# Down projection of a two-layer decoder trunk: first pass in half units with one pair at its end, second pass with its squares behind the next unit's parts, and the scale row on SP's queue

## Chip, core and metric

The kernel runs on one core of one Trainium2 chip, as one program and one launch. The metric is the device time of that launch in microseconds (us); lower is better. The core's engines are PE (matmuls; PEld is its weight load), DVE (vector), ACT (scalar), POOL (GpSimd) and SP, which here only issues DMAs. Each engine takes its own instructions in order, and semaphores tie the engines together.

## The reference, cut to what matters

Two layers, 512 tokens of width 1024, all in float32. Layer 0 mixes tokens by trailing means, layer 1 by attention over a window of 128 keys; after each stands the same feed-forward part, and this is what the change touches:

```python
def rms_norm(x, g):
    y = xf * lax.rsqrt(jnp.mean(xf * xf, axis=-1, keepdims=True) + RMS_EPS)
    return y * g

def conv_glu_ffn(h, w_in, conv_w, conv_b, w_out):      # h: (512, 1024)
    u = h @ w_in                                       # (512, 5632)
    up = jnp.pad(u, ((0, 0), (CONV_WIDTH - 1, 0), (0, 0)))
    u = sum(conv_w[k] * up[:, k:k + S] for k in range(3)) + conv_b
    gate, val = jnp.split(u, 2, axis=-1)
    return (gelu(gate) * val) @ w_out                  # (512, 2816) @ (2816, 1024)

for layer in range(2):
    h = rms_norm(x, mix_pre_g[layer])
    if layer == 0:
        m = pool_mixer(h, w_pool, pool_scale)          # ends with: y * scale, a row of 1024
    else:
        m = attention(h, ...)
    x = x + rms_norm(m, mix_post_g[layer])
    x = x + rms_norm(conv_glu_ffn(rms_norm(x, ffn_pre_g[layer]), ...), ffn_post_g[layer])
```

## The kernel before, in words

**Every product is three matmuls.** A float32 operand is cut into a high part (a copy to the format fp32r, on ACT) and a low part (the operand minus the high part, on DVE). `mm3` (L322 to L325) then issues high by high (L323), one low by high (L324) and the other low by high (L325). So each block of weights that lands in a buffer `raw` needs a cast on ACT (`wh`, L236) and a subtraction on DVE (`wl`, L237) before PE may use it. `split(i)` does this for weight unit i in two halves of 1024 columns and then asks SP to load units i+1 and i+2 into the two `raw` buffers. Three slots hold `wh`/`wl`; a few units of the second pass have a slot of their own (`homes`).

**The feed-forward part of a layer** runs in three stages. `first` makes the up projection for 22 column blocks j: 48 matmuls each, then `act(j)`, in which `conv` runs on ACT (L540) and DVE (L541, L542) for the gate half `tg`, then Gelu on ACT (L549), then `conv` for the value half `tv`, then their product (L556). Two blocks make a pair p; there are 11 pairs.

The down projection multiplies by a scheme of seven products in place of eight. Sums of quarters of the activations (`g_sums`) and of the weights (`w_sums`, written to DRAM as `t`) are made on POOL during `first`. **`pass1`** makes the products named 1, 6, 5 and 7, eight PSUM banks in all. Pair p uses unit `U_D1 + p` (four blocks of 512 columns, one for each product) and the activation parts `gh`, `gl` of `split1(p)`: a subtraction on DVE (L580), a cast on ACT (L582, `gh`), a subtraction on DVE (L583, `gl`). `gh` and `gl` rotate through five buffers `w4`, so `gl` of pair p+2 takes the buffer of `gh` of pair p. The loop runs over pairs 0 to 8 (`NP - NT` with `NT = 2`): `split1(p + 2)`, 24 matmuls, then `ahead(U_D1 + p)`, which splits unit p+2. The last two pairs stand together: product 1 of pairs 9 and 10, then product 6 of both, and so on.

**`pass2`** makes product 4 (three units m, 11 pairs) and then products 3 and 2 (six units, 11 pairs, the last three pairs one bank after the other). `soon(k)` splits the k-th of these nine units and makes its activation parts (`split2`, L654 on ACT and L655 on DVE). Between them stand the sums `Z` on DVE (L670, L722), the squares for the norm on ACT (`square_of`, L255), their sum and root on POOL (`root`), the gains on DVE (L697) and the new residual (`update`, L707). In layer 0 the norm of the next layer's input follows for blocks 2 and 3 (`pre_a`, `pre_b`) and their transposes on PE (`to_attention`).

**At the start**, the row of 1024 pool scales is loaded into partition 0 of a buffer `row` that DVE has filled with zeros (L88), and four matmuls with ones (L355) spread it over the partitions. The DMA is issued on ACT's queue (L333), behind half of `band`. Blocks x0 and x1 of the input are loaded by SP and normed by ACT, DVE and POOL (L366 to L374) before PE pools them (L394 to L397).

PE, ACT, DVE and POOL run in the order in which the code is written; SP's order is chosen by the framework.

## Time and profile before

| what | value |
|---|---|
| three timed runs | 919.35, 920.88, 922.05 us (median 920.88) |
| profiled execution | 920.7 us, span 918.9 us: 1.8 us lie around the span |
| instructions on PE (matmuls) | 4700 |
| `pass1` of layer 0, `pass2` of layer 0 | from 280.25 us, from 341.99 us |
| attention stage | from 390.88 us |
| `pass1` of layer 1, `pass2` of layer 1 | from 805.61 us, from 866.48 us; last matmul ends at 911.5 us |

A row of the timeline reads: start in us, duration in us, engine, line, operation, what is written and from what, shapes, count, and in brackets the idle time of that engine ahead of it with what ended the idle time. The end of a matmul is modelled in this profile: 128x512 matmuls that start 0.23 us apart are listed with 0.39 us each, so a busy PE is read by the distances between starts. In the prediction "layer 0" and "layer 1" are the two feed-forward parts, and units and pairs carry the numbers of the section above.

### The profile page before, as it was taken

How to read it: one execution, taken by the hardware profiler on the slowest of the kernel's cores; microseconds unless marked ns; L12 is line 12 of the kernel's file. 1: busy time of each engine (PE TensorE's matmuls, PEld its weight loads, DVE VectorE, ACT ScalarE, POOL GpSimd, SP SyncE). 2: the span in 40 equal slices, each digit the busy share in tenths (PEclk: the TensorE clock that was granted, in tenths of full speed). 3: DMA queues.
4: the chain of work that ended last, by engine and by line, in shares of the span. 5: the costliest groups of instructions: out<-in, count | busy, mean ns of one | idle time of the engine just before them, and what ended most of it. 6: DMA issues, size and time to landing. Idle time of an engine off the chain costs nothing.

```text
span 918.9 us, 12766 instructions
## 1 busy us (share of the span) xinstructions
PE 905.4 (99%) x4700; PEld 775.7 (84%) x4700; DVE 643.3 (70%) x958; ACT 465.2 (51%) x811; POOL 323.0 (35%) x371
## 2 busy tenths in 40 slices
PE   9999999999999999999999999999999999999996
PEld 8998888888887878799999889988888888888785
DVE  5878877677677777854888737655555555677877
ACT  5644444445344655554888634433433333455562
POOL 3415444444341000234767212544433333410001
PEclk9999999999999999999999999999999999999999
DMA  8356797888884655742112243455555555456643
GB/s 312 131 192 232 290 313 253 298 293 302 270 290 142 198 203 184 292 148 87 47 47 93 92 162 137 155 217 190 193 202 200 196 187 195 159 169 192 225 169 114
DMA packets 45184, 178.49 MB, mean 194 GB/s; under 512 B 5313, under 2 KB 6849, under 8 KB 36930
## 3 DMA queue, kind: packets, MB, share of 16 engines
q1 hardware_dynamic: 42720, 164.57, 50.9%
q10 hardware_dynamic: 2402, 13.11, 3.7%
q8 instruction: 37, 0.61, 0.3%
q14 instruction: 25, 0.20, 0.1%
HBM read 139.91 MB, written 37.75 MB: 193 GB/s over the span
## 4 chain that ended last, share of the span: by engine, by line
PE 82%; DVE 7%; issue 3%; DMA 3%; ACT 3%; POOL 2%; POOLq 0%; DVEq 0%; SPq 0%; ACTq 0%
PE u L325 17%; PE u L324 17%; PE u L323 17%; PE dn L324 4%; PE dn L325 4%; PE dn L323 4%; DVE wl L237 3%; DMA raw<-t 2%; PE qp L323 2%; PE qp L324 2%; PE qp L325 2%; PE op L323 2%; PE op L325 2%; PE op L324 2%; PE pT L929 1%
## 5 line engine op out<-in xcount | busy, mean ns | idle before, releaser
L323 PE MATMUL u<-xTh_f,wh 128*128 128x512 f32 (+1 forms) x768 | 285.7, 372 | 0.0
L324 PE MATMUL u<-xTl_f,wh 128*128 128x512 f32 (+1 forms) x768 | 285.2, 371 | 0.0
L325 PE MATMUL u<-xTh_f,wl 128*128 128x512 f32 (+1 forms) x768 | 285.2, 371 | 0.0
L237 DVE TENSOR_TENSOR wl<-raw,wh 128x1024 fp32r<-128x1024 f32 (+1 forms) x158 | 206.7, 1349 | 15.8 <-ACT wh L236 15.6
L541 DVE SCALAR_TENSOR_TENSOR t<-u,conv,t 128x511 f32<-128x511 f32 x88 | 65.8, 747 | 145.1 <-ACT t L540 145.1
L324 PEld LDWEIGHTS u<-xTl_f,wh 128*128 128x128 f32 x768 | 144.7, 188 | 25.1
L323 PEld LDWEIGHTS u<-xTh_f,wh 128*128 128x128 f32 x768 | 144.7, 188 | 24.9
L325 PEld LDWEIGHTS u<-xTh_f,wl 128*128 128x128 f32 x768 | 144.6, 188 | 24.8
L236 ACT CAST wh<-raw 128x1024 fp32r<-128x1024 f32 (+1 forms) x158 | 156.8, 1041 | 12.0 <-DMA raw<-t 7.5
L540 ACT ACTIVATE t<-u,conv 128x512 f32<-128x512 f32 x88 | 68.3, 777 | 139.0 <-PE u L325 104.9
L561 POOL TENSOR_TENSOR G<-G,G 128x256 f32<-128x256 f32 x22 | 33.4, 1516 | 266.2 <-DVE G L556 266.2
L324 PE MATMUL dn<-wl,gh 128*128 128x512 f32 x276 | 107.9, 391 | 1.8 <-DVE wl L237 1.8
L325 PE MATMUL dn<-wh,gl 128*128 128x512 f32 x276 | 107.8, 390 | 1.2 <-DVE gl L655 1.1
L323 PE MATMUL dn<-wh,gh 128*128 128x512 f32 x276 | 107.7, 390 | 0.0
L549 ACT ACTIVATE t<-t 128x512 f32<-128x512 f32 x44 | 27.8, 633 | 104.3 <-DVE t L542 104.3
L542 DVE SCALAR_TENSOR_TENSOR t<-u,conv,t 128x510 f32<-128x510 f32 x88 | 65.9, 749 | 3.1
L324 PEld LDWEIGHTS dn<-wl,gh 128*128 128x128 f32 x276 | 51.8, 188 | 14.0 <-DVE wl L237 3.4
L325 PEld LDWEIGHTS dn<-wh,gl 128*128 128x128 f32 x276 | 51.8, 188 | 12.9 <-DVE gl L655 2.4
L323 PEld LDWEIGHTS dn<-wh,gh 128*128 128x128 f32 x276 | 51.8, 188 | 11.0 <-ACT gh L654 0.3
L257 POOL TENSOR_SCALAR ss_p_f<-ss_p_f 128x1 f32<-128x1 f32 x8 | 3.2, 400 | 161.2 <-ACT dn L255 161.2
L582 ACT CAST gh<-G 128x1024 fp32r<-128x1024 f32 x22 | 23.1, 1051 | 56.0 <-DVE G L580 43.6
L583 DVE TENSOR_TENSOR gl<-G,gh 128x1024 fp32r<-128x1024 f32 x22 | 27.5, 1250 | 26.2 <-ACT gh L582 19.9
(199 smaller groups left out, 1517.5 us busy)
## 6 DMA issues: line engine op xcount, KB each, us to landing
raw<-in_ws_dram SPq DMA_DIRECT2D x48, 1024.0 KB, 5.0
q<-in_ws_dram SPq DMA_DIRECT2D x44, 512.0 KB, 6.4
raw<-t SPq DMA_DIRECT2D x24, 768.0 KB, 5.5
raw<-in_ws_dram SPq DMA_DIRECT2D x24, 512.0 KB, 4.6
t<-q SPq DMA_DIRECT2D x44, 256.0 KB, 3.0
t<-q SPq DMA_DIRECT2D x22, 512.0 KB, 3.0
r<-in_ws_dram SPq DMA_DIRECT2D x12, 512.0 KB, 6.9
hi<-h SPq DMA_DIRECT2D x12, 512.0 KB, 6.6
```

Source lines behind the costliest of these rows:

```text
L236: nc.scalar.copy(hi[:, s], r[:, s])
L237: nc.vector.tensor_tensor(lo[:, s], r[:, s], hi[:, s].bitcast(F32), ALU.subtract)
L323: nc.tensor.matmul(acc, ah, bh, start=first, stop=False)
L324: nc.tensor.matmul(acc, ah, bl, start=False, stop=False)
L325: nc.tensor.matmul(acc, al, bh, start=False, stop=last)
L540: nc.scalar.activation(t, u, AF.Identity, bias=conv_col(l, ch, 3), scale=conv_col(l, ch, 2))
L541: nc.vector.scalar_tensor_tensor(t[:, 1:], u[:, : S - 1], conv_col(l, ch, 1), t[:, 1:], ALU.mult, ALU.add)
L542: nc.vector.scalar_tensor_tensor(t[:, 2:], u[:, : S - 2], conv_col(l, ch, 0), t[:, 2:], ALU.mult, ALU.add)
L549: nc.scalar.activation(tg, tg, AF.Gelu_apprx_tanh)
L561: nc.gpsimd.tensor_tensor(s1, s1, G2[:, p, 2, :], ALU.add)
L582: nc.scalar.copy(h, G1[:, o : o + 1024])
L583: nc.vector.tensor_tensor(lo, G1[:, o : o + 1024], h.bitcast(F32), ALU.subtract)
```

## The change

Five edits; no instruction is added on PE, ACT, DVE or POOL.

- `split(i, between)` can call a function between its two halves. `split1(p, unit)` uses it: the order is now sum (L580), first half of the unit, `gh` and `gl`, second half of the unit, and all of it stands ahead of the 24 matmuls of pair p-2.
- `pass1` ends with one pair (`NT = 1`): pairs 0 to 9 run one after the other, and pair 10 alone stands at the end. `ahead` is gone from the loop.
- `conv` of the value half: the first step (ACT) of `tv` stands ahead of the Gelu of `tg`.
- `pass2`: the square of `Z22[m]` stands after `soon(m + 3)` in place of ahead of it; `soon(5)` stands ahead of the sums and squares of `Z21`, and `soon(6)` ahead of the gains.
- The DMA of the scale row is issued by SP, third in its queue, ahead of `cst`, x1 and the second part of `band`.

```diff
-    def split(i):
+    def split(i, between=None):
         if i in slots or i >= N_UNITS:
+            if between:
+                between()
             return
...
             nc.scalar.copy(hi[:, s], r[:, s])
             nc.vector.tensor_tensor(lo[:, s], r[:, s], hi[:, s].bitcast(F32), ALU.subtract)
+            if between and o == 0:
+                between()
...
+    nc.sync.dma_start(row[0:1], a["pool_scale"])
     nc.sync.dma_start(cst[:, :C_LATE], a["cst"][:, :C_LATE])
     nc.sync.dma_start(x[1], a["x"][1])
-    nc.scalar.dma_start(row[0:1], a["pool_scale"])
...
-        def conv(t, u, ch):
+        def conv(t, u, ch, then=lambda: None):
             nc.scalar.activation(t, u, AF.Identity, ...)
+            then()
...
             conv(tg, accs[j][0], j)
-            nc.scalar.activation(tg, tg, AF.Gelu_apprx_tanh)
-            conv(tv, accs[j][1], NF + j)
+            conv(tv, accs[j][1], NF + j, lambda: nc.scalar.activation(tg, tg, AF.Gelu_apprx_tanh))
...
-        def split1(p):
+        def split1(p, unit=None):
...
-            nc.scalar.copy(h, G1[:, o : o + 1024])
-            nc.vector.tensor_tensor(lo, G1[:, o : o + 1024], h.bitcast(F32), ALU.subtract)
+            def parts():
+                nc.scalar.copy(h, G1[:, o : o + 1024])
+                nc.vector.tensor_tensor(lo, G1[:, o : o + 1024], h.bitcast(F32), ALU.subtract)
+            if unit is None:
+                parts()
+            else:
+                split(unit, parts)
...
-        NT = 2
+        NT = 1
...
         for p in range(NP - NT):
-            split1(p + 2)
+            if p + 2 < NP:
+                split1(p + 2, U_D1[l] + p + 2)
             for q in of:
                 make(q, p)
-            ahead(U_D1[l] + p)
...
             soon(m + 2)
+            if m:
+                square_of("22", m - 1, 7)
             if m < 2:
                 nc.vector.tensor_tensor(Z["22"][m], Z["12"][m], X[7][m], ALU.add)
                 add("21", m, 7)
-                square_of("22", m, 7)
...
             if p == 0:
+                soon(5)
                 for i in range(2):
                     add("21", i, 4)
                     square_of("21", i, 4)
                     root(2 + i)
-                soon(5)
+                soon(6)
                 for i in range(2):
                     gain("21", i)
-                soon(6)
```

On PE, at the end of `pass1` of layer 0 (`dn_1_1` is the second bank of product 1, `dn_6_0` the first of product 6; `gh_9` and `gh_10` are the parts of pairs 9 and 10), there stood before:

```order
L325 MATMUL dn_1_1_2396<-wh_2698,gl_9_2671 128x512
L323 MATMUL dn_1_0_2395<-wh_2735,gh_10_2707 128x512
L324 MATMUL dn_1_0_2395<-wl_2736,gh_10_2707 128x512
L325 MATMUL dn_1_0_2395<-wh_2735,gl_10_2708 128x512
L323 MATMUL dn_1_1_2396<-wh_2735,gh_10_2707 128x512
```

and now stands:

```order
L330 MATMUL dn_1_1_2396<-wh_2672,gl_9_2671 128x512
L328 MATMUL dn_6_0_2397<-wh_2672,gh_9_2670 128x512
L329 MATMUL dn_6_0_2397<-wl_2673,gh_9_2670 128x512
L330 MATMUL dn_6_0_2397<-wh_2672,gl_9_2671 128x512
L328 MATMUL dn_6_1_2398<-wh_2672,gh_9_2670 128x512
```

The first use of pair 10 moved 18 matmuls back.

On ACT, in `pass2` of layer 0 from the parts of the last unit of product 4 (`gh_0_2` of 768 columns) on (`wh` rows are weight units, `gh_0_0` and `gh_0_1` the parts of the first two units of products 3 and 2, the `ACTIVATE` rows the squares), there stood before:

```order
L654 CAST gh_0_2_2867<-G_0_724 128x768
L255 ACTIVATE dn_7_0_2401,ss_p_f_2873<-Z_0_2797 128x512
L236 CAST wh_2900<-raw_2821 128x1024 x2
L654 CAST gh_0_0_2909<-G_0_724 128x1024
L255 ACTIVATE dn_7_1_2402,ss_p_f_2915<-Z_0_2797 128x512
L236 CAST wh_2936<-raw_2864 128x1024 x2
L654 CAST gh_0_1_2945<-G_0_724 128x1024
L255 ACTIVATE dn_4_0_2828,ss_p_f_2873<-Z_0_2797 128x512
L255 ACTIVATE dn_4_1_2829,ss_p_f_2915<-Z_0_2797 128x512
L236 CAST wh_2971<-raw_2906 128x1024 x2
L654 CAST gh_0_2_2980<-G_0_724 128x1024
```

and now stands:

```order
L666 CAST gh_0_2_2867<-G_0_724 128x768
L239 CAST wh_2897<-raw_2821 128x1024 x2
L666 CAST gh_0_0_2906<-G_0_724 128x1024
L260 ACTIVATE dn_7_0_2401,ss_p_f_2910<-Z_0_2797 128x512
L239 CAST wh_2933<-raw_2864 128x1024 x2
L666 CAST gh_0_1_2942<-G_0_724 128x1024
L260 ACTIVATE dn_7_1_2402,ss_p_f_2946<-Z_0_2797 128x512
L239 CAST wh_2963<-raw_2903 128x1024 x2
L666 CAST gh_0_2_2972<-G_0_724 128x1024
L260 ACTIVATE dn_4_0_2828,ss_p_f_2910<-Z_0_2797 128x512
L260 ACTIVATE dn_4_1_2829,ss_p_f_2946<-Z_0_2797 128x512
```

Each square moved behind one more unit's casts.

On DVE, in the loop of `pass1` of layer 0 (`gl_8` and `gl_9` are low parts of activations, `G_0` rows the sums of L580, `wl` rows the low parts of weight units 8 and 9), there stood before:

```order
L580 TENSOR_TENSOR G_0_728<-G_0_724,G_0_728 128x256
L583 TENSOR_TENSOR gl_8_2633<-G_0_728,gh_8_2632 128x1024
L237 TENSOR_TENSOR wl_2661<-raw_2590,wh_2660 128x1024 x2
L580 TENSOR_TENSOR G_0_728<-G_0_724,G_0_728 128x256
L583 TENSOR_TENSOR gl_9_2671<-G_0_728,gh_9_2670 128x1024
L237 TENSOR_TENSOR wl_2699<-raw_2628,wh_2698 128x1024 x2
```

and now stands:

```order
L585 TENSOR_TENSOR G_0_728<-G_0_724,G_0_728 128x256
L240 TENSOR_TENSOR wl_2635<-raw_2566,wh_2634 128x1024
L590 TENSOR_TENSOR gl_8_2633<-G_0_728,gh_8_2632 128x1024
L240 TENSOR_TENSOR wl_2635<-raw_2566,wh_2634 128x1024
L585 TENSOR_TENSOR G_0_728<-G_0_724,G_0_728 128x256
L240 TENSOR_TENSOR wl_2673<-raw_2604,wh_2672 128x1024
L590 TENSOR_TENSOR gl_9_2671<-G_0_728,gh_9_2670 128x1024
L240 TENSOR_TENSOR wl_2673<-raw_2604,wh_2672 128x1024
```

The low part of the activations moved between the two halves of the unit.

## The prediction, made before the run

> **What bounds the kernel now.** I read the page first, for the engine that carries the span, then PE's starts in the four stages that the change touches, then what DVE and ACT do where PE waits.
>
> ```profile
> span 918.9 us, 12766 instructions
> PE 905.4 (99%) x4700; PEld 775.7 (84%) x4700; DVE 643.3 (70%) x958; ACT 465.2 (51%) x811; POOL 323.0 (35%) x371
> PE 82%; DVE 7%; issue 3%; DMA 3%; ACT 3%; POOL 2%; POOLq 0%; DVEq 0%; SPq 0%; ACTq 0%
> ```
>
> PE carries 82% of the chain that ended last. No matmul is added or taken away, so time can only come out of stretches in which PE's starts are spread. The busy time by stretches, for the matmuls of the down projection alone, shows them: `pass1` and `pass2` of layer 0, then of layer 1.
>
> ```profile
> core 0: us, PE busy (x) PEld busy (x) DVE busy (x) ACT busy (x), PEclk, DMA share, GB/s
> 280.25:341.99 61.74, 60.68 (x264) 49.31 (x264) 1.28 (x2) 1.06 (x2) 1.00 0.59 189
> 341.99:390.88 48.89, 46.46 (x199) 36.52 (x197) 6.37 (x10) 4.12 (x12) 1.00 0.64 234
> 805.61:866.48 60.87, 60.16 (x265) 49.47 (x264) 1.28 (x2) 1.06 (x2) 1.00 0.56 188
> 866.48:911.40 44.92, 44.92 (x199) 36.97 (x197) 7.16 (x11) 4.96 (x14) 1.00 0.44 152
> ```
>
> The last row is dense: its 11 pairs are 198 matmuls (one more is counted at an edge), so one takes 44.92 / 198 = 0.2269 us, at a granted clock of 1.00. A `pass1` has 264 matmuls, 59.9 us when dense. It took 61.74 and 60.87: **1.84 and 0.97 us** are waits. `pass2` of layer 0 took 48.89, 3.97 more than its dense twin; two groups of transposes, 0.78 each, belong to it,
>
> ```profile
> 380.05 1.03 PE L316 MATMUL tr_a<-cst,xn_a 128*128 128x128 f32 x8
> 380.83 0.48 PE L323 MATMUL dn<-wh,gh 128*128 128x512 f32 x1
> ```
>
> which leaves **2.4 us**. Together 5.2 us is what the edits in the down projection can win at most, 0.57% of the kernel. Where it lies, from PE's timeline:
>
> ```profile
> 292.08 0.50 PE L324 MATMUL dn<-wl,gh 128*128 128x512 f32 x1 [0.35 <-DVE wl L237]
> 331.44 0.39 PE L323 MATMUL dn<-wh,gh 128*128 128x512 f32 x1
> 332.54 0.50 PE L324 MATMUL dn<-wl,gh 128*128 128x512 f32 x1 [0.71 <-DVE wl L237]
> 857.03 0.50 PE L324 MATMUL dn<-wl,gh 128*128 128x512 f32 x1 [0.71 <-DVE wl L237]
> 368.19 0.40 PE L324 MATMUL dn<-wl,gh 128*128 128x512 f32 x1
> 369.48 0.50 PE L325 MATMUL dn<-wh,gl 128*128 128x512 f32 x1 [0.89 <-DVE gl L655]
> 381.76 0.50 PE L325 MATMUL dn<-wh,gl 128*128 128x512 f32 x1 [0.21 <-DVE gl L655]
> ```
>
> Each is a wait for a low part from DVE. The second pair of rows shows how to read them: from start to start 1.10 us in place of 0.23, so 0.87 lost, though the bracket says 0.71. The brackets add up to 2.9 us, the starts to 5.2; I go by the starts. The Trainium skill (Perfetto Trace Analysis, section Identifying the Most-Contended Engine) tells the reader to find the gaps between slices of the bounding engine: by that rule the prize is 2.9 us and the sum below would end near 918, but the same page (section Per-instruction lifecycle) calls the end of a matmul's slice an estimate, and here 0.39 us are listed for starts 0.23 apart, so the distances of this trace decide.
>
> **`pass1`, the loop.** No instruction is added; what moves is the order on DVE and ACT. Before, one pair reads:
>
> ```profile
> 298.07 0.42 DVE L580 TENSOR_TENSOR G<-G,G 128x256 f32<-128x256 f32 x1
> 299.65 1.23 DVE L583 TENSOR_TENSOR gl<-G,gh 128x1024 fp32r<-128x1024 f32 x1 [1.16 <-ACT gh L582]
> 300.79 2.35 DVE L237 TENSOR_TENSOR wl<-raw,wh 128x1024 fp32r<-128x1024 f32 x2
> 298.56 1.05 ACT L582 CAST gh<-G 128x1024 fp32r<-128x1024 f32 x1 [2.04 <-PE dn L325]
> 299.52 2.00 ACT L236 CAST wh<-raw 128x1024 fp32r<-128x1024 f32 x2
> ```
>
> DVE idles 1.16 us for `gh`, so a pair costs it 0.42 + 1.16 + 1.14 + 2.27 = 5.0 us by starts, against 24 x 0.2269 = 5.45 on PE. Now the first half of the unit stands in that hole: 1.14 of work covers the 1.05 of `gh`, a pair costs about 3.9 us, and `wl` of the first half comes ahead of `gl`. `gl` itself comes 1.14 later in the order; behind it stand the second half and, on PE, the third matmul of pair p+2, which comes a whole pair (5.45 us) after the buffer of `gl` is free, so the delay is hidden.
>
> The wait at 292.08 is DVE being late out of `first`:
>
> ```profile
> 282.54 0.75 DVE L541 SCALAR_TENSOR_TENSOR t<-u,conv,t 128x511 f32<-128x511 f32 x1 [1.43 <-ACT t L540]
> 289.66 1.23 DVE L583 TENSOR_TENSOR gl<-G,gh 128x1024 fp32r<-128x1024 f32 x1 [1.18 <-ACT gh L582]
> ```
>
> The `conv` edit takes away most of the 1.43 (ACT's first step for `tv` no longer waits behind Gelu, whose result DVE needs only for the product after it), and the first half of unit 2 no longer waits for the 1.18 and the 1.23. Together some 3.8 us earlier, for a wait of 0.67: gone. A small wait at the start of pair 1 (0.2) goes with the 1.43. In the rest of `first` the `conv` edit is worth nothing, since PE does not wait there.
>
> **`pass1`, the end.** The waits at 332.54 and 857.03 are pair 10 being used six matmuls after pair 9 begins, while its parts could not be made sooner:
>
> ```profile
> 330.13 1.23 DVE L583 TENSOR_TENSOR gl<-G,gh 128x1024 fp32r<-128x1024 f32 x1 [1.37 <-PE dn L324]
> 331.27 2.35 DVE L237 TENSOR_TENSOR wl<-raw,wh 128x1024 fp32r<-128x1024 f32 x2
> ```
>
> `gl` of pair 10 needs the buffer that PE leaves at the end of pair 8, and `wl` stood behind it. With `NT = 1` pair 10 comes 18 matmuls, 4.1 us, later, and `wl` stands ahead of `gl`: both waits go. What the two pairs together covered is the start of `pass2`: product 1 was complete 36 matmuls before the end, now 18, 4.1 us. ACT's two copies out of its banks take 1.1 us and stand behind the casts of the next unit anyway, so this is hidden; without the cover it would cost about 1 us a layer. **Term: -1.84 and -0.97**, ends 0 and -2.8 together.
>
> **`pass2` of layer 0.** The wait at 369.48 (369.48 - 368.19 - 0.23 = 1.06, and some refill around it) is the low part of `soon(5)`:
>
> ```profile
> 362.85 1.27 DVE L670 TENSOR_TENSOR Z<-Z,dn 128x512 f32<-128x512 f32 x2
> 365.92 2.36 DVE L237 TENSOR_TENSOR wl<-raw,wh 128x1024 fp32r<-128x1024 f32 x2 [1.80 <-ACT wh L236]
> 368.20 1.22 DVE L655 TENSOR_TENSOR gl<-G,gh 128x1024 fp32r<-128x1024 f32 x1
> 363.62 0.60 ACT L255 ACTIVATE dn<-Z 128x512 f32<-128x512 f32 x1 [3.52 <-DVE Z L670]
> 364.86 1.99 ACT L236 CAST wh<-raw 128x1024 fp32r<-128x1024 f32 x2
> ```
>
> The casts of the unit stood on ACT behind two squares, which stood behind two sums on DVE, which then idled 1.80 us. Now `soon(5)` goes first: DVE starts it near 362.9 of the old clock, 3.0 us earlier, against 1.3 us of wait and a PE that arrives 1.84 earlier. That alone is a close thing; the two moved squares of `Z22` take two more idle stretches of DVE off the same queue, of which I count on half. The waits at 381.76 and after it are the units behind the norm of block 2:
>
> ```profile
> 377.42 0.88 DVE L301 TENSOR_SCALAR xn_a<-x,ss_n_a 128x512 f32<-128x512 f32 x2 [0.74 <-POOL ss_n_a L264]
> 378.22 2.35 DVE L237 TENSOR_TENSOR wl<-raw,wh 128x1024 fp32r<-128x1024 f32 x2
> 380.49 1.22 DVE L655 TENSOR_TENSOR gl<-G,gh 128x1024 fp32r<-128x1024 f32 x1
> ```
>
> Here DVE is full, and its work is the same as before. `gl` ended at 381.71. It gains at least the 1.80 of idle time, giving 379.9; PE arrives 1.84 + 1.3 = 3.1 earlier, at 378.3, and would wait 1.6. With the idle time ahead of the two `Z22` units gone too, it would not wait. I take 0.4 left. **Term: -2.0**, ends -0.8 and -2.4. `pass2` of layer 1 has no wait to lose; the squares moved there are covered by a dense PE.
>
> **The scale row.** ACT issued it at 2.09, and SP would have to hold its queue until DVE's zeros are there, about then.
>
> ```profile
> 2.09 0.50 ACTq L333 DMA_DIRECT2D row<-in_pool_scale_dram  x1
> 1.64 0.61 SPq L331 DMA_DIRECT2D cst<-in_cst_dram  x1
> 7.08 0.63 ACT L366 ACTIVATE xm<-x 128x512 f32<-128x512 f32 x1 [2.83 <-DMA x<-in_x_dram]
> 4.00:5.00 1.00, 0.74 (x5) 0.58 (x4) 0.06 (x1) 0.26 (x2) 0.00 (x0) 1.00 0.97 309
> ```
>
> `cst` would be issued at 2.6 in place of 1.64, and x1 behind it as much later, 0.95 us. x1 is on the path: ACT waits for it at 7.08 and PE for what follows. But the DMA engines are 0.97 busy then, so x1 waits for its turn and not for its issue. I take 0, with ends -0.1 and +0.95. The Trainium skill (DMA: Bandwidth & Descriptors, section Issuing engines are not separate DMA queues) says that issuing from several engines saves only the initiating time. It speaks against this edit: by it ACT is spared 0.50 us that nothing waits for, SP pays it, and the sum would end 0.5 higher if x1 followed its issue; the 0.97 of this trace says that it need not.
>
> **Sum.** -1.84 - 0.97 - 2.0 + 0 = -4.8 us. Against the profiled execution, 920.7 us (its span of 918.9 and 1.8 around it), that gives **915.9 us**; the median of the runs is 920.88, so the two bases agree within 0.2. It is 0.5%, where 0.3%, about what a measurement of this kernel can tell from no change, is 2.8 us.
>
> **The rivals.**
> - DVE, not the order, bounds `pass2` of layer 0: only the 1.80 of idle time comes off, so layer 0 ends 1.8 earlier whatever `pass1` wins, and layer 1 gives 0.97: 917.9. For it: the full rows at 377 to 382. Against it: three idle stretches ahead of them, not one.
> - x1 follows its issue and PE starts 0.95 later, the rest as forecast: 916.8.
> - The edits do not do what they say: the waits at the end of `pass1` are set by loads, not by order, and come back one pair later; `pass2` as in the first rival: about 920. Against it: both brackets name DVE, and DVE's own wait there named PE.
> - Slower: the ring of loads in `pass1`. Unit p+4 is loaded into the buffer that the second half of unit p+2 leaves, and that half now stands behind `gl`.
>
> ```profile
> raw<-t SPq DMA_DIRECT2D x24, 768.0 KB, 5.5
> DMA to landing us min/median/max: 3.8/4.8/7.4
> ```
>
> The ring is 0.4 (the first of two issues) + 5.5 + 1.05 + 1.14 + 1.14 + 1.22 = 10.5 us for two pairs, where PE takes 10.9; before it was 1.14 shorter. If landings are 7.4 like the longest, it is 12.4, 1.5 too long, 4.5 times in a pass, less some 3 us of lead: 3.8 in each layer. The waits in `pass1` that went then do not count, `pass2` still gives 2.0, and the kernel takes 920.7 + 7.6 - 2.0 = 926. It decides from a mean landing of about 7.0.
>
> **How the numbers follow.** Forecast 0.66; DVE bound 0.15; x1 late 0.08; loads set the end 0.07; ring of loads 0.04. Faster by over 0.3%, below 918.1: the forecast but for 0.02, x1, and half of the DVE case: 0.80. Within 0.3%: the rest of these and the fourth case, 0.16. Slower: the ring, 0.04. The bounds of the forecast's own terms go from -5.3 to -3.0 when the worst ends of two do not meet; the runs scatter by 1.4 us to either side. The range from 914.2 to 918.9 leaves out the last two cases and a little at the bottom.
>
> **What the profile after would show.** Right: `pass1` of both layers near 59.9 us; no wait for `wl` at their ends; `pass2` of layer 0 near 46.9 with DVE's idle time ahead of `soon(5)` gone; x1 landing near 7.1. Wrong: new brackets for `raw` on ACT inside `pass1`; a PE wait for `gl` before the last three pairs as long as what `pass1` won; a late start of the pooling at 9.69 us and after.

## The result, and the profile after

| kernel | runs | median | range |
|---|---|---|---|
| before | 5 | 920.88 us | 919.35 to 922.05 |
| changed | 5 | 915.38 us | 915.17 to 916.32 |

The ratio is 0.9949, with a 95% interval from 0.9937 to 0.9960: the change makes the kernel 0.5% faster. The profiled execution of the changed kernel took 915.99 us, 4.7 less than that of before (920.7).

From the page of the changed kernel, the span, the engines' busy time and the chain that ended last:

```profile
span 914.2 us, 12802 instructions
PE 903.6 (99%) x4700; PEld 776.5 (85%) x4700; DVE 643.3 (70%) x958; ACT 463.2 (51%) x811; POOL 337.5 (37%) x371
PE 93%; DVE 2%; POOL 1%; ACT 1%; issue 1%; DMA 0%; POOLq 0%; DVEq 0%; ACTq 0%
```

DVE's busy time is the same 643.3 us as before. The same work is done; PE's share of the chain went from 82 to 93%, because the steps over DVE, DMA and ACT, 13% of it before, are down to 3%. The four stages, by the windows of the changed kernel for the down projection's tile (`pass1` and `pass2` of layer 0, then of layer 1; the lines that stand against 61.74, 48.89, 60.87 and 44.92):

```profile
core 0: us, PE busy (x) PEld busy (x) DVE busy (x) ACT busy (x), PEclk, DMA share, GB/s
280.72:340.56 59.84, 59.84 (x264) 49.55 (x264) 1.27 (x2) 1.05 (x2) 1.00 0.61 195
340.56:387.26 46.70, 45.44 (x199) 36.83 (x197) 6.38 (x10) 4.11 (x12) 1.00 0.66 249
801.95:861.79 59.84, 59.84 (x265) 49.55 (x264) 1.28 (x2) 1.06 (x2) 1.00 0.58 188
861.79:906.73 44.94, 44.94 (x199) 36.97 (x197) 7.16 (x11) 4.94 (x14) 1.00 0.45 155
```

Both `pass1` are dense. The list of all waits of PE in the changed kernel (in all, times, longest) has no row for `dn` any more:

```profile
engine line waited for: us in total, times, longest us
PE tr_f L321 <- DVE xn_f L313: 1.3, 2, 0.9
PE scratch L355 <- DVE warm L85: 1.0, 1, 1.0
PE scale_row L360 <- DMA row<-in_pool_scale_dram: 0.5, 1, 0.5
PE kt L861 <- ACT kst L855: 0.2, 1, 0.2
PE kp L330 <- DVE xTl_a L325: 0.2, 1, 0.2
```

The table gives the account of the 4.7 us, and below it the same for the experiments. It is made from the starts of PE's matmuls in each profiled execution: "head" is the start of the first up-projection matmul, a stage lasts from its first matmul to the first of the next (the last one to the start of the last matmul). Everything between these stages was the same within 0.1 us in all executions.

| kernel | head | `pass1`, layer 0 | `pass2`, layer 0 | `pass1`, layer 1 | `pass2`, layer 1 | span |
|---|---|---|---|---|---|---|
| before | 37.08 | 61.74 | 48.89 | 60.87 | 44.65 | 918.9 |
| changed | 37.57 | 59.84 | 46.70 | 59.84 | 44.65 | 914.2 |
| difference | +0.49 | -1.90 | -2.19 | -1.03 | 0 | -4.7 |
| before_one_pair | 39.90 | 60.69 | 48.01 | 59.84 | 45.21 | 919.2 |
| end_two_pairs | 37.27 | 63.57 | 46.70 | 64.15 | 44.65 | 922.0 |
| parts_first | 39.56 | 59.84 | 46.70 | 59.84 | 44.65 | 916.2 |
| gl_twice | 37.95 | 64.21 | 47.39 | 63.85 | 44.65 | 923.7 |
| gelu_first | 37.16 | 60.87 | 46.70 | 59.84 | 44.65 | 914.9 |
| second_pass_old | 37.79 | 59.84 | 49.26 | 59.84 | 45.77 | 918.1 |
| soon_old | 37.29 | 59.84 | 46.70 | 59.84 | 44.65 | 913.9 |
| squares_old | 37.24 | 60.19 | 51.98 | 59.84 | 46.63 | 921.6 |
| row_on_act | 39.31 | 59.84 | 46.70 | 59.84 | 44.65 | 916.0 |
| as_changed | 37.81 | 59.84 | 46.70 | 59.84 | 44.65 | 914.4 |
| warm_first | 37.20 | 59.84 | 46.70 | 59.84 | 44.65 | 913.8 |
| three_edits | 37.84 | 59.84 | 46.70 | 59.84 | 44.65 | 914.5 |

### The profile page after: what moved, and what is told of

Its sections match the earlier page's. It is cut to its first block, busy times and chain, and to the rows that moved or that the text cites. A ratio compares the mean times of both kernels' runs of the same rounds, so it can differ in the third digit from the quotient of the medians.

```text
span 914.2 us, 12802 instructions
## 1 busy us (share of the span) xinstructions
PE 903.6 (99%) x4700; PEld 776.5 (85%) x4700; DVE 643.3 (70%) x958; ACT 463.2 (51%) x811; POOL 337.5 (37%) x371
## 4 chain that ended last, share of the span: by engine, by line
PE 93%; DVE 2%; POOL 1%; ACT 1%; issue 1%; DMA 0%; POOLq 0%; DVEq 0%; ACTq 0%
PE u L328 17%; PE u L330 17%; PE u L329 17%; PE dn L330 7%; PE dn L328 7%; PE dn L329 7%; PE qp L328 2%; PE qp L329 2%; PE qp L330 2%; PE op L328 2%; PE op L329 2%; PE op L330 2%; PE pT L943 1%; PE s L908 1%; PE s L907 1%; PE qt L886 1%
## 5 line engine op out<-in xcount | busy, mean ns | idle before, releaser
L239 ACT CAST wh<-raw 128x1024 fp32r<-128x1024 f32 (+1 forms) x158 | 158.9, 1042 | 53.4 <-DMA raw<-t 38.3
L262 POOL TENSOR_SCALAR ss_p_f<-ss_p_f 128x1 f32<-128x1 f32 x8 | 18.5, 2316 | 156.4 <-ACT dn L260 156.4
L328 PE MATMUL qp<-wh,xTh_a 128*128 128x256 f32 x128 | 36.5, 285 | 0.0
L329 PE MATMUL qp<-wl,xTh_a 128*128 128x256 f32 x128 | 36.2, 283 | 0.0
L330 PE MATMUL qp<-wh,xTl_a 128*128 128x256 f32 x128 | 36.2, 282 | 0.0
```

The lines of the kernel that those rows point to most:

```text
L239: nc.scalar.copy(hi[:, s], r[:, s])
L262: nc.gpsimd.tensor_scalar(ss[:, h : h + 1], ss[:, h : h + 1], EPS, None, ALU.add)
L328: nc.tensor.matmul(acc, ah, bh, start=first, stop=False)
L329: nc.tensor.matmul(acc, ah, bl, start=False, stop=False)
L330: nc.tensor.matmul(acc, al, bh, start=False, stop=last)
```

## The experiments

Each kernel was timed beside the kernel before on the same chip. Most are the changed kernel with one edit taken back.

### The first pass

**before_one_pair**: the kernel before, with the single pair at the end and nothing else.

```diff
-        NT = 2
+        NT = 1
         for p in range(NP - NT):
-            split1(p + 2)
+            if p + 2 < NP:
+                split1(p + 2)
```

> The kernel before with one pair at the end of the first pass in place of two, and nothing else changed. Theory 1 (pair 10 was used too early): the waits at 332.5 and 857.0 us go, the first pass of layer 0 takes 60.8 us in place of 61.74 and that of layer 1 59.84 in place of 60.87; the second pass of layer 0 keeps its waits and PE comes to it 1 us earlier, so up to 1 us is given back there; 919.0 to 920.0 us against 920.9. Theory 2 (the order of halves is needed as well, since the unit of pair 10 still stands behind the low part of its activations): at least half of both waits stays, each 0.4 us or more.

Measured: 920.38 us against 920.30, ratio 0.9997 (0.9986 to 1.0007). The stages bear out theory 1: `pass1` of layer 1 is dense, and that of layer 0 has lost the wait at its end and keeps the one at its start, PE's only `dn` wait there in this kernel's timeline:

```profile
294.86 0.50 PE L324 MATMUL dn<-wl,gh 128*128 128x512 f32 x1 [0.31 <-DVE wl L237]
```

So the single pair alone is worth 1.05 and 1.03 us in `pass1`. Of the second, 0.56 is given back in `pass2` of layer 1, which had no wait before. In `pass2` of layer 0 nothing is given back, against the expectation: it is 0.88 us shorter. There the two executions differ in one load, that of the first unit of `pass2`, for which ACT waits (the kernel before, then this one):

```profile
335.90 2.00 ACT L236 CAST wh<-raw 128x1024 fp32r<-128x1024 f32 x2 [4.10 <-DMA raw<-t]
336.53 2.00 ACT L236 CAST wh<-raw 128x1024 fp32r<-128x1024 f32 x2 [1.91 <-DMA raw<-t]
```

It was issued 291.37 us after the head in both, and landed 7.4 us after its issue in the kernel before and 5.2 us after it here; DVE, measured from the head, reaches `soon(5)` 1.97 us earlier here, PE `pass2` only 1.07. So some of the wait at 369.48 us, on which the prediction builds, belongs to one slow load of one execution. The time did not follow the stages: this execution lost 2.8 us at its head (below). By its stages the kernel should gain about 2.4 us on the profile of before, and only its fastest run (918.29, 2.0 below the median beside it) comes near that; why the others don't is open.

**end_two_pairs**: the changed kernel with two pairs at the end.

```diff
-        NT = 1
+        NT = 2
```

> The changed kernel with two pairs at the end of the first pass (NT = 2) in place of one. Theory 1 (as the prediction put it: pair 10 comes too early for its parts): waits of 0.5 to 1 us come back at the end of both first passes, on the low part of the activations of pair 10, which needs the buffer that PE leaves at the end of pair 8; each first pass takes 60.3 to 60.9 us and the kernel about 916.5 to 917. Theory 2 (the order of the halves alone does it, since the low part of the unit now stands ahead): both first passes stay at 59.84 us and the kernel at 915.4.

Measured: 921.73 us against 920.06, ratio 1.0008 (0.9995 to 1.0021). Theory 1 holds in kind and falls far short in size: each `pass1` is 3.7 to 4.3 us longer in the profile. That execution (923.77) is the slowest of the 12 runs; the fastest five took 918.74 to 919.94, some 2.6 to 3.8 above the changed kernel's 916.11 (as_changed). PE's and ACT's timelines of this kernel at the end of `pass1` of layer 0:

```profile
330.55 0.39 PE L330 MATMUL dn<-wh,gl 128*128 128x512 f32 x1
331.77 0.50 PE L328 MATMUL dn<-wh,gh 128*128 128x512 f32 x1 [0.83 <-ACT gh L589]
332.11 0.48 PE L329 MATMUL dn<-wl,gh 128*128 128x512 f32 x1
333.23 0.50 PE L330 MATMUL dn<-wh,gl 128*128 128x512 f32 x1 [0.63 <-DVE gl L590]
333.56 0.47 PE L328 MATMUL dn<-wh,gh 128*128 128x512 f32 x1
333.83 0.63 PE L329 MATMUL dn<-wl,gh 128*128 128x512 f32 x1
334.25 0.63 PE L330 MATMUL dn<-wh,gl 128*128 128x512 f32 x1
```

```profile
329.73 1.05 ACT L239 CAST wh<-raw 128x1024 fp32r<-128x1024 f32 x1 [1.47 <-DMA raw<-t]
330.69 1.04 ACT L589 CAST gh<-G 128x1024 fp32r<-128x1024 f32 x1
```

The cast `gh` of pair 10 now stands behind the cast of half a unit, and that one waited 1.47 us for its load. So the high part is late too, which no wait of PE at this place named in the kernel before. PE loses 0.99 us at 331.77 (1.22 from start to start) and 0.89 at 333.23. Then it goes on at 0.43 us a matmul in place of 0.227. The windows of this kernel have the granted clock behind the engines' busy times:

```profile
core 0: us, PE busy (x) PEld busy (x) DVE busy (x) ACT busy (x) POOL busy (x), PEclk, DMA share, GB/s
332.00:333.00 1.00, 0.60 (x2) 0.19 (x1) 1.00 (x2) 0.67 (x1) 0.00 (x0) 1.00 1.11 434
333.00:334.00 1.00, 0.77 (x3) 0.65 (x4) 1.00 (x2) 0.00 (x0) 0.00 (x0) 0.87 0.78 328
334.00:335.00 1.00, 1.00 (x4) 0.81 (x3) 0.31 (x1) 0.00 (x0) 0.00 (x0) 0.50 0.09 25
335.00:336.00 1.00, 1.00 (x4) 0.72 (x4) 0.00 (x0) 0.00 (x0) 0.00 (x0) 0.50 0.76 131
336.00:337.00 1.00, 1.00 (x4) 0.81 (x3) 0.00 (x0) 0.25 (x1) 0.00 (x0) 0.50 0.86 328
337.00:338.00 1.00, 1.00 (x6) 0.83 (x5) 0.17 (x1) 1.00 (x2) 0.00 (x0) 0.93 1.00 426
```

By the clock, 0.13 + 3 x 0.50 + 0.07 = 1.7 us of work are lost here, nearly as much as the two waits that came before. Sum: 0.99 + 0.89 + 1.7 = 3.6 of the 3.73 us.

**parts_first**: the changed kernel with `gh` and `gl` ahead of the whole unit, as before.

```diff
-                split(unit, parts)
+                parts()
+                split(unit)
```

> The changed kernel with both parts of the activations ahead of the whole unit in the first pass, as before, where the change put them between its halves. Theory 1 (DVE's idle time of 1.16 us for every pair was hidden, since 5.0 us a pair lie below PE's 5.44, and the halves only make the ring of loads 1.14 us longer): both first passes stay at 59.84 us, or at most 0.2 longer at their start, and the casts of the units wait less for loads; 915.2 to 915.6 in all. Theory 2 (the halves took the waits at 292 us and at the ends away, together with the single pair): the first pass of layer 0 takes 60.3 to 60.9 us, a wait for the low part of unit 2 or 3 is back, and the kernel takes 915.9 to 916.5.

Measured: 916.07 us, where the changed kernel beside it (as_changed) took 916.11; against the kernel before 0.9957 (0.9942 to 0.9973). Theory 1: every stage is the same to 0.01 us, so **the halves are worth nothing** beside the single pair and the conv edit. ACT's timeline of this kernel in the loop:

```profile
304.82 1.05 ACT L589 CAST gh<-G 128x1024 fp32r<-128x1024 f32 x1 [2.05 <-DVE G L585]
309.83 1.05 ACT L589 CAST gh<-G 128x1024 fp32r<-128x1024 f32 x1 [2.05 <-DVE G L585]
```

A pair takes DVE and ACT 5.01 us, and ACT waits for DVE, not for loads. That is below PE's 5.44, so DVE's idle time was never felt.

**gl_twice**: the changed kernel, with 1.14 us more on DVE between the halves.

```diff
-                nc.vector.tensor_tensor(lo, G1[:, o : o + 1024], h.bitcast(F32), ALU.subtract)
+                for _ in range(2 if unit is not None else 1):
+                    nc.vector.tensor_tensor(lo, G1[:, o : o + 1024], h.bitcast(F32), ALU.subtract)
```

> The changed kernel with the low part of the activations of pairs 2 to 10 in the first pass made twice, one after the other, so 1.14 us more on DVE between the two halves of a unit. Theory 1 (the rival of the prediction, the ring of loads: half unit, low part, half unit, load, cast, with a period measured as 10.67 us for two pairs where PE takes 10.88): the period grows to 11.8 us, PE waits 0.9 us for every two pairs once its lead is used up, and each first pass takes 1 to 4 us longer; 918 to 923 in all. Theory 2 (DVE's own count sets the pace: 3.9 + 1.14 = 5.0 us a pair against 5.44 on PE): no wait in the loop, both first passes at 59.84 us, 915.4.

Measured: 925.38 us against 920.30, ratio 1.0053 (1.0040 to 1.0066). Theory 1 in kind, and above its range of 1 to 4 us a pass and 918 to 923 in all: 4.4 and 4.0 us for the two `pass1`. ACT's casts of units in the changed kernel come first, then PE's waits with `gl` made twice:

```profile
292.81 1.05 ACT L239 CAST wh<-raw 128x1024 fp32r<-128x1024 f32 x1 [2.97 <-DMA raw<-t]
303.48 1.05 ACT L239 CAST wh<-raw 128x1024 fp32r<-128x1024 f32 x1 [2.90 <-DMA raw<-t]
313.98 1.05 ACT L239 CAST wh<-raw 128x1024 fp32r<-128x1024 f32 x1 [2.67 <-DMA raw<-t]
```

```profile
311.07 0.50 PE L330 MATMUL dn<-wh,gl 128*128 128x512 f32 x1 [1.34 <-DVE gl L591]
322.96 0.50 PE L330 MATMUL dn<-wh,gl 128*128 128x512 f32 x1 [0.67 <-DVE gl L591]
334.75 0.50 PE L330 MATMUL dn<-wh,gl 128*128 128x512 f32 x1 [0.57 <-DVE gl L591]
```

In the changed kernel the ring of loads turns in 10.67 and 10.50 us for two pairs, 0.2 to 0.4 below PE's 10.88. With 1.14 more in it PE's waits come every 11.89 and 11.79 us. DVE's own count, 5.0 us a pair, would still have fitted.

**gelu_first**: the changed kernel with Gelu ahead of ACT's first step for the value half.

```diff
-            conv(tv, accs[j][1], NF + j, lambda: nc.scalar.activation(tg, tg, AF.Gelu_apprx_tanh))
+            nc.scalar.activation(tg, tg, AF.Gelu_apprx_tanh)
+            conv(tv, accs[j][1], NF + j)
```

> The changed kernel with the Gelu of the gate half ahead of ACT's first step for the value half, as before. Theory 1 (as predicted: PE waits in the first stage of the feed-forward part nowhere, and at its end the halves of the units cover the 1.4 us): no change, first pass of layer 0 at 59.84 us, 915.4 in all. Theory 2 (the conv edit is what took the waits at 286 and 292 us away): the first pass of layer 0 takes 60.1 to 60.7 us and the kernel 915.7 to 916.3.

Measured: 916.71 us against 920.06, ratio 0.9964 (0.9952 to 0.9976). Theory 2, a little above its range: `pass1` of layer 0 takes 60.87. 0.18 us are lost at its start; the rest is one wait in the middle, on PE and on ACT in this kernel's timeline:

```profile
308.87 0.50 PE L330 MATMUL dn<-wh,gl 128*128 128x512 f32 x1 [0.53 <-DVE gl L591]
```

```profile
305.37 1.05 ACT L239 CAST wh<-raw 128x1024 fp32r<-128x1024 f32 x1 [3.87 <-DMA raw<-t]
```

One load landed 6.7 us after its issue where those around it took 5.5 to 5.7, and DVE, which without the conv edit comes out of `first` 1.2 us later against PE's start, had no lead to cover it: PE lost 0.81. This part is one slow load of one execution. With the edit the lead is there: in as_changed and three_edits the load at the same place took 6.4 us, in end_two_pairs 6.8, and PE lost nothing behind it; in squares_old it took 7.1, and PE lost 0.29. The wait at 292 us does not come back, so the halves alone remove that one. The conv edit alone removes it as well: before_one_pair, without the edit and the halves, has 60.69, and parts_first, with the edit and without the halves, 59.84.

### The second pass

Three kernels: the changed one with the second pass as before (**second_pass_old**), with only units 5 and 6 moved back (**soon_old**), and with only the squares of `Z22` moved back (**squares_old**). The first has both edits below, the others one each.

```diff
             if p == 0:
-                soon(5)
                 for i in range(2):
                     add("21", i, 4)
                     square_of("21", i, 4)
                     root(2 + i)
-                soon(6)
+                soon(5)
                 for i in range(2):
                     gain("21", i)
+                soon(6)
```

```diff
             soon(m + 2)
-            if m:
-                square_of("22", m - 1, 7)
             if m < 2:
                 nc.vector.tensor_tensor(Z["22"][m], Z["12"][m], X[7][m], ALU.add)
                 add("21", m, 7)
+                square_of("22", m, 7)
```

> The changed kernel with the second pass in the order of before: squares of Z22 ahead of the next unit's parts, units 5 and 6 behind the sums and gains of Z21. Theory 1 (the order on ACT and DVE makes the waits, and PE now comes 1.9 us earlier than before while DVE's work is as late): the second pass of layer 0 takes 48.9 to 50.8 us in place of 46.7, with the wait for the low part of unit 5 grown from 1.3 us by up to 1.9, and the kernel 917.6 to 919.5. Theory 2 (the waits came from the first pass, whose lateness was carried over): it stays near 46.7 us, the kernel at 915.4. The second pass of layer 1 stays at 45.04 us by both.

> The changed kernel with units 5 and 6 of the second pass behind the sums and gains of Z21 again; the squares of Z22 stay where the change put them. Theory 1 (the place of unit 5 is what makes the wait of 1.3 us): the wait for its low part is back with 1.3 us or more and the second pass of layer 0 takes 48 to 49.5 us in place of 46.7; 916.7 to 918.2 in all. Theory 2 (the two idle stretches of DVE ahead of the Z22 squares were what made DVE late): below 47.2 us, 915.4 to 915.9.

> The changed kernel with the squares of Z22 ahead of the next unit's parts again; units 5 and 6 stay ahead of the sums and gains. Theory 1 (the place of unit 5 is enough, as it stands ahead of both squares of Z21): the second pass of layer 0 takes 46.7 to 47.0 us, 915.4 to 915.7 in all. Theory 2 (the close thing of the prediction: without the two idle stretches PE catches up with DVE): DVE idles twice by about 1.7 us again, and PE waits for the low parts of units 4 and 5, or of those behind the norm of block 2, by 0.5 to 2 us; 915.9 to 917.4.

| kernel | median | before beside it | ratio |
|---|---|---|---|
| second_pass_old | 921.02 us | 920.06 us | 1.0015 (1.0006 to 1.0024) |
| soon_old | 915.71 us | 920.30 us | 0.9951 (0.9938 to 0.9964) |
| squares_old | 921.71 us | 920.30 us | 1.0007 (0.9996 to 1.0018) |

second_pass_old: theory 1 in layer 0 (49.26). Both theories missed layer 1, which takes 1.12 us longer (45.77 for 44.65; the expectation's 45.04 is the same stage to the end of its last matmul): with PE 1.03 earlier, the stage that had no wait has one. soon_old: theory 1 fell, theory 2 is exact; **the place of units 5 and 6 is worth nothing**. squares_old: theory 2 in kind, and worse than it allowed, 5.28 us in layer 0 and 1.98 in layer 1. The times agree with the stages: without the squares' move the whole gain is gone.

DVE's timeline shows why, first of the changed kernel, then of squares_old (the rows on which DVE idled between 346 and 372 us):

```profile
364.10 2.36 DVE L240 TENSOR_TENSOR wl<-raw,wh 128x1024 fp32r<-128x1024 f32 x2 [1.75 <-ACT wh L239]
```

```profile
352.21 2.36 DVE L240 TENSOR_TENSOR wl<-raw,wh 128x1024 fp32r<-128x1024 f32 x2 [1.73 <-ACT wh L239]
358.63 2.36 DVE L240 TENSOR_TENSOR wl<-raw,wh 128x1024 fp32r<-128x1024 f32 x2 [1.73 <-ACT wh L239]
369.67 2.36 DVE L240 TENSOR_TENSOR wl<-raw,wh 128x1024 fp32r<-128x1024 f32 x2 [1.74 <-ACT wh L239]
```

A square on ACT waits for DVE's sum, the next unit's casts stand behind the square, and DVE waits for the casts. Moving unit 5 ahead of `Z21` does not remove such a stretch; it moves it one unit on, to unit 6. The move of the `Z22` squares removes the other two, 3.46 us. With all three left in this execution of squares_old, and the third of them late, DVE reaches the full stretch behind the norm of block 2 late, and PE waits once for long (PE's timeline of squares_old, then its windows):

```profile
382.10 0.50 PE L330 MATMUL dn<-wh,gl 128*128 128x512 f32 x1 [1.77 <-DVE gl L667]
```

```profile
382.00:384.00 2.00, 1.90 (x7) 1.21 (x8) 2.00 (x4) 0.95 (x2) 1.51 (x2) 0.85 1.02 430
384.00:386.50 2.50, 2.50 (x6) 1.98 (x7) 1.77 (x4) 0.00 (x0) 0.00 (x0) 0.50 1.01 426
```

The wait is 2.04 us by starts, and again the granted clock is halved behind it: 2.50 x 0.50 + 2.00 x 0.15 = 1.6 us more, and some of the next window. In second_pass_old PE's longest wait in this stage is 1.07 us by starts (0.9 in its bracket) and the clock stays. The 2.72 us between the two profiles are not the price of an edit alone. In `pass1`, where the two kernels are the same, ACT waited longer for a load in squares_old (first row) than in second_pass_old:

```profile
326.34 1.05 ACT L239 CAST wh<-raw 128x1024 fp32r<-128x1024 f32 x1 [4.06 <-DMA raw<-t]
325.19 1.05 ACT L239 CAST wh<-raw 128x1024 fp32r<-128x1024 f32 x1 [2.96 <-DMA raw<-t]
```

That load took 7.0 us in squares_old and 5.8 in second_pass_old, and the first two idle stretches of DVE, which stand in the same order in both, come 1.26 us later in squares_old. Its profile is also the slowest of 12 runs, that of second_pass_old the fastest of 11; the medians are only 0.69 us apart. In layer 1 squares_old lost 1.98 us and second_pass_old 1.12, with loads of the usual length in both. What this shows is that moving units 5 and 6 does not help while the squares stay where they were; how much it harms is open.

### The head

**row_on_act**: the changed kernel with the row's DMA on ACT's queue, where it was before.

```diff
-    nc.sync.dma_start(row[0:1], a["pool_scale"])
     nc.sync.dma_start(cst[:, :C_LATE], a["cst"][:, :C_LATE])
     nc.sync.dma_start(x[1], a["x"][1])
+    nc.scalar.dma_start(row[0:1], a["pool_scale"])
```

> The changed kernel with the DMA of the scale row issued by ACT again, everything else as changed. Theory 1 (the move itself costs): the row is issued about 1 us earlier, lands earlier, the four matmuls that spread it start near 4.97 us in place of 5.29 and the first of them takes 0.50 and not 0.99 us; the first up-projection matmul starts near 37.1 in place of 37.57, and the kernel takes about 914.9 against 915.4. Theory 2 (the 0.49 us at the head is a difference between two executions, as landings scatter): the first up-projection matmul stays anywhere from 37.1 to 37.6 and the time within 0.3 us of 915.4. All stages behind the head stay: first passes 59.84 us, second pass of layer 0 46.7 us.

**as_changed**: no edit.

> The changed kernel once more, without any edit, as the measure for the two kernels beside it on this chip. Theory 1 (only the head differs between executions of this kernel, since it has no wait in the first and second passes): first passes 59.84 us, second passes 46.70 and 44.65 us as in the first profile; the first up-projection matmul anywhere from 37.1 to 38.0 us; 915.2 to 916.3 in the runs. Theory 2 (the ring of loads has so little slack that a single slow landing shows): one first pass longer by 0.2 to 1 us.

**warm_first**: the changed kernel, with all warming products ahead of the row.

```diff
-    keep_busy(8)
+    keep_busy(12)
     for h in range(2):
         nc.tensor.matmul(scale_row[h], warm, row[:, h * 512 : (h + 1) * 512], start=True, stop=True)
-    keep_busy(4)
```

> The changed kernel with all 12 warming products ahead of the four matmuls that spread the scale row, where 8 stood ahead and 4 behind: the same work on PE, but no wait for the row in the middle of the warming. Theory 1 (at the head PE runs at half speed until it has worked some 3.5 us without a pause, and the wait of 0.3 to 1.2 us for the row puts this off by 1 to 4 us): the first matmul of the row takes 0.50 us or less in place of 0.99, pooling starts at 7.5 to 7.7 us in place of 8.49, the first up-projection matmul near 37.1, and the kernel takes 914.6 to 915.2. Theory 2 (the pace at the head is set by the landings of x0 and x1): the first up-projection matmul where it is beside it, within 0.2 us, and the time the same.

| kernel | median | range | before beside it | ratio |
|---|---|---|---|---|
| row_on_act | 916.33 us | 915.64 to 919.15 | 920.06 us | 0.9962 (0.9948 to 0.9976) |
| as_changed | 916.11 us | 915.64 to 916.55 | 919.86 us | 0.9953 (0.9935 to 0.9972) |
| warm_first | 916.05 us | 915.63 to 916.18 | 919.86 us | 0.9952 (0.9935 to 0.9968) |

The rows of the changed kernel at the head that answer to those of before, from the timeline (SP's issues of the row and of x1, and ACT's first use of x1):

```profile
2.08 0.30 SPq L336 DMA_DIRECT2D row<-in_pool_scale_dram  x1
2.83 0.43 SPq L338 DMA_DIRECT2D x<-in_x_dram  x1
6.88 0.63 ACT L371 ACTIVATE xm<-x 128x512 f32<-128x512 f32 x1 [2.60 <-DMA x<-in_x_dram]
```

row_on_act: theory 1 fell. Its head was not 0.5 us shorter but 1.7 longer (39.31, which theory 2's range misses too), so the +0.49 of the first profile can't be read as the price of the move. as_changed: theory 1; its passes are the same to 0.01 us and its head is 37.81. Its use of x1 came 1.29 us later than in the first profile, though the kernel is the same:

```profile
8.17 0.63 ACT L371 ACTIVATE xm<-x 128x512 f32<-128x512 f32 x1 [3.93 <-DMA x<-in_x_dram]
```

warm_first: the rows of theory 1 came out (the row's matmuls 0.43 us apart, pooling at 7.67, head 37.20), its time did not: the median is 0.06 us beside that of as_changed, within the scatter, as theory 2 had it.

What makes the head long in some executions is PE's pace. The four matmuls of the row in PE's timeline, of the changed kernel, of parts_first (head 39.56) and of warm_first:

```profile
5.29 2.48 PE L360 MATMUL scale_row<-row,warm 128*128 128x512 f32 x4 [0.47 <-DMA row<-in_pool_scale_dram]
```

```profile
5.62 3.75 PE L360 MATMUL scale_row<-row,warm 128*128 128x512 f32 x4 [0.80 <-DMA row<-in_pool_scale_dram]
```

```profile
5.95 1.88 PE L360 MATMUL scale_row<-row,warm 128*128 128x512 f32 x4
```

The same four matmuls take 1.88, 2.48 or 3.75 us in these rows. In parts_first the last three are 0.85 us apart, twice the 0.43 of the others. The three profiles in which this happened (parts_first, row_on_act, before_one_pair) are those with heads of 39.3 to 39.9 us. In all three a wait for the row had interrupted the warming, but so it did, by 0.3 to 0.8 us, in executions with a short head: the wait alone does not decide it. Of the runs of kernels whose passes have no waits, 5 of 31 with 8 warming products ahead of the row were above 917 us, and none of 11 with 12 ahead. That points to a use of warm_first, and is too few runs to show it.

The smaller spread of the heads goes with x1. In the three profiles in which ACT used x1 only after 8 us (gl_twice, second_pass_old, as_changed) the head is 37.79 to 37.95; in the five in which x1 came between 7.0 and 7.6 us (end_two_pairs, gelu_first, soon_old, squares_old, warm_first) it is 37.16 to 37.29. The changed kernel's first profile, 37.57 with x1 at 6.88, does not fit this; there pooling began at 8.49 us, in those five at 7.62 to 8.16.

### What is enough

**three_edits**: three of the edits (single pair, squares of `Z22`, conv) and the warming of warm_first. Against the kernel before (left out: the unit is split whole behind both parts, which in the code now stands ahead of the 24 matmuls):

```diff
-    keep_busy(8)
+    keep_busy(12)
...
-    keep_busy(4)
...
-            nc.scalar.activation(tg, tg, AF.Gelu_apprx_tanh)
-            conv(tv, accs[j][1], NF + j)
+            conv(tv, accs[j][1], NF + j, lambda: nc.scalar.activation(tg, tg, AF.Gelu_apprx_tanh))
...
-        NT = 2
+        NT = 1
...
+            if m:
+                square_of("22", m - 1, 7)
...
-                square_of("22", m, 7)
```

> The kernel before with three of the change's edits alone (one pair at the end of the first pass, the squares of Z22 behind the next unit's parts, ACT's first step for the value half ahead of the Gelu), and with all 12 warming products ahead of the scale row; units are split whole behind both parts of the activations, units 5 and 6 stand behind the sums and gains, and ACT issues the row. Theory 1 (these edits carry the whole gain, the halves, the move of units 5 and 6 and the row's queue nothing): first passes 59.84 us, second passes 46.70 and 44.65 us, the first up-projection matmul at 37.0 to 37.4 us, 915.4 to 916.1 in the runs, and none above 917, since PE's clock does not drop at the head. Theory 2 (an edit left out matters when another that covered it is gone too): a wait of 0.3 us or more in a first or second pass, 916.3 or more.

Measured: 916.14 us (916.03 to 916.29) against 919.66, ratio 0.9955 (0.9940 to 0.9970). Theory 1, but for its head and so for a few tenths (37.84: DVE began on its half of x0 at 5.70 us, in the changed kernel at 5.00). All four passes are those of the changed kernel, so the other edits carry nothing in them beside these three. It is no faster than the changed kernel, which took 915.38 and 916.11.

## Why the prediction was right, and where it was not

The forecast was 915.9 us from 920.7; the profiled execution took 915.99 and the median is 915.38. The sum was -4.8; the profiles give -4.7. That the two agree to 0.1 is in part luck: the medians give -5.5 in the first measurement and -3.75 in the second (as_changed), since the kernel before scatters by 3 to 5 us, and its profile holds one load of 7.4 us.

- **`pass1`, -1.84 and -0.97**: measured -1.90 and -1.03. The single pair brings 1.05 and 1.03 of it, as the step for the end of `pass1` said. The other 0.85 goes with the conv edit, and without it some waits stay: 0.18 at the start and 0.81 behind a slow load (gelu_first). What the steps put beside these was not needed: "`wl` stands ahead of `gl`" and "the first half of unit 2 no longer waits" name the halves, and parts_first has the same 59.84 without them.
- **`pass2` of layer 0, -2.0**: measured -2.19, for another reason than the step gave. "It gains at least the 1.80 of idle time" failed: that stretch was moved from unit 5 to unit 6, where it is 1.75. The two stretches at the `Z22` squares, "of which I count on half", were all that the edits won. The size came out by luck: 3.46 us of idle time gone is about as much as 1.80 and half of 3.46. The 2.19 also holds an unknown part that no edit won, the slow load of the profile of before: before_one_pair, with the second pass as before and a load of 5.2 us, is 1.31 above the changed kernel. Of the working by the order of engines, the fault was to follow one wait to its idle stretch and to move that, without asking where the same circle (sum, square, cast, low part) would close next.
- **`pass2` of layer 1, 0**: right, but "covered by a dense PE" was not the reason. Without the squares' move this stage loses 1.12 us (second_pass_old) or 1.98 (squares_old), more than its `pass1` wins. The step asked in layer 0 what a PE that comes earlier would meet, and not in layer 1.
- **The scale row, 0**: no effect of the move can be told from the scatter, so the term is not refuted, and its reason is not shown. In the first profile x1 was issued 0.54 us later (2.83 against 2.29) and ACT used it 0.20 earlier (6.88 against 7.08), as the step had it. In as_changed, the same kernel, it was 1.09 later (8.17), beyond the bound of +0.95. Over all profiles ACT used x1 at 6.88 to 8.17 us where SP issued the row (ten, mean 7.56), at 7.08 to 7.84 where ACT did (four, mean 7.42). The Trainium skill (DMA: Bandwidth & Descriptors, section Issuing engines are not separate DMA queues) says that DMAs of all issuing engines run on the same 16 DMA engines; with this scatter the runs here neither confirm nor contradict it. Whether the SP queue makes the head better or worse on the mean stays open: with 8 warming products ahead of the row, its heads were 37.16 to 37.95 in eight profiles and 39.56 in one, those on ACT's queue 37.08, 39.31 and 39.90.
- **The rivals**: the ring of loads did not decide, and its arithmetic held: 10.5 estimated, 10.67 and 10.50 measured, and gl_twice, with 11.89 and 11.79 against PE's 10.88, shows the predicted kind of loss, 4.0 to 4.4 us a pass. The halves brought the kernel within 0.4 us of that point for no gain. Something like "DVE bounds `pass2`" is seen in squares_old: with the idle stretches left, and a slow load ahead of them, the full rows behind the norm make PE wait.
- **Price of a wait**: the prediction summed waits as lost starts. That holds for those of before: the three stages that changed gave back 5.1 of the 5.2 us that it read there by the starts, where the brackets had 2.9. (The advice on gaps between slices that it names from the Trainium skill stands, in Perfetto Trace Analysis, under Optimization Strategy.) It does not hold for a wait of 2.0 us, or for 1.0 and 0.9 in short order, where a second loss follows (squares_old, end_two_pairs).

## What to carry to other kernels

Where two engines wait for each other in a circle, move the one piece that breaks the circle; a unit that is only put ahead of it hands the idle stretch to the next. An engine's idle time inside a loop that is paced by another engine is no prize, and filling it can tighten a ring of buffers that had slack: work out the ring's period beside the engine's count. When a stage is made faster, ask of every later stage what PE meets when it arrives earlier, also where it meets nothing now.

## What the runs showed of the hardware

- Pauses of PE of 1.9 us within 3 us (end_two_pairs), and one of 2.0 us (squares_old), were followed by 3 to 4 us at a granted clock of 0.50, with starts 0.43 us apart in place of 0.227. The drop comes up to 1.3 us after the pause is over (squares_old: work goes on at 382.10, starts slow down after 383.4). The waits of 1.1 us of the kernel before left the clock at 1.00, and so did single ones of 1.5 us (gl_twice at 311.07 us, squares_old at 905.84). The Trainium skill (TensorE: Matmul & The Clock Gate, section HAM oscillation — how this bites in real kernels) puts the rule at gaps above some 3.4 us; here 2.0 us in one piece, or 1.9 in two, were followed by the drop.
- At the head of three profiles the distances are doubled too (0.85 us for a matmul of the row that otherwise takes 0.43), while the granted clock in the windows reads 1.00 there. That this is the same drop of the clock is likely and not shown; the distances are the safer reading.
- Kernels with waits in their passes scatter more than those without: 918.7 to 923.6 us for the kernel before on one chip, where as_changed beside it has 915.64 to 916.55. In end_two_pairs the drop of the clock has a part in this: five runs of 918.7 to 919.9 us have a mean granted clock of 0.997 to 0.998, seven of 921.6 to 923.8 us one of 0.994 to 0.997. In the kernel before it has none that can be seen: its runs at 0.997 took 918.9 to 923.1 us, those at 0.998 918.6 to 923.6. Slow loads, as the one of 7.4 us in its profile, would do it; with one execution profiled this is not shown.
